# One 512-wide product for the tokens' hi and lo parts in the first layers of an MLP and two FFNs

## The chip, the cores and the metric

The kernel runs on one core of a Trainium2 chip. The metric is the device time of one execution in microseconds. TensorE multiplies (PE in the profile; its weight loads are PEld), VectorE is DVE, ScalarE is ACT, GpSimd is POOL, and SP issues the weights' transfers.

## What is computed

Two transformer blocks on 256 tokens of 1024 features, in float32. The parts of the reference that the change touches are an MLP at the end of the first block and two gated layers (FFNs) at the start and the end of the second:

```python
ff = jnp.square(jax.nn.relu(u2 @ mlp_w1[layer])) @ mlp_w2[layer]      # 1024 -> 4096 -> 1024
h = h + gate2 * ff

def swiglu(x, w_gu, w_down):                                         # 1024 -> 2 x 2816 -> 1024
    g, u = jnp.split(x @ w_gu, 2, axis=-1)
    return (jax.nn.silu(g) * u) @ w_down
x = x + 0.5 * swiglu(rmsnorm(x, ffn1_norm[l]), ffn1_w_gu[l], ffn1_w_down[l])
```

## The kernel before

**Arithmetic.** Each float32 operand of a large product is split into a hi part (rounded to TensorE's fp32r type) and a lo part (the rest). A product of two operands is the sum of three: hi by hi, hi by lo, lo by hi.

**The weight stream.** Class `Stream` brings all weights in order of use, in transfers of at most 2048 columns, into a ring of three raw tiles, and cuts them into pieces of 128 x 1024. A piece's hi part is an ACT copy (L342), its lo part a DVE subtraction (L330). There is room for six split pieces. After each piece of products `done` gives its room back and `fill` splits pieces up to four ahead.

**Order of the work.** Every engine works through its instructions in the order in which the program writes them. TensorE's order is written out by hand. An instruction that needs a tile's buffer waits until the last user of the tile that had it before is done.

**PSUM.** There are eight banks of 512 columns: a0 to a3, w0, w1, t0 and t1. `wbank()` deals out w0 and w1 in turn, `tbank()` t0 and t1 in turn, over the whole program. Five `wbank` calls and an even number of `tbank` calls stand ahead of the MLP.

**The three stages.** In the MLP and in each FFN the first layer gives the hidden features, 128 at a time (one piece of weights), for all 256 tokens; `lin_A` makes a piece from eight blocks of 128 features, three 256-wide products each. Two pieces share a bank: features 2p and 2p + 1 in the MLP, gate and up of one j in an FFN. The pair is then emptied (`relu2`, `hidden`), split into hi and lo, and three pairs (MLP) or four (FFN) later its second-layer products, 512 wide, go into a0 to a3 (`down_tile`, and at the end `down_tail`). The first four pieces (MLP) or two pairs (FFN) of a stage are made the other way round, by `lin_B`, token tile 0 first, into two banks from `wbank()`; their result lies token by token and is transposed behind the stage's first pair, L1369 to L1375 and L1447 to L1454. The head's results in the MLP lie in tiles with the tag `r`, which has two buffers; so does the `r` of `relu2`.

**Work between.** Class `Background` puts small steps of other chains between the products, by a planned clock in microseconds of TensorE that counts 5.2 for a pair and 2.6 for a second-layer piece. In the MLP these are the norm of the memory with four groups of transpositions (`mem_norm`, L1273), in the first FFN the memory's keys (`mem_keys`, two groups, L1324). They take banks from `tbank()`.

**The tokens' parts.** `new_xT` gives two tiles of 128 x 8 x 256, one for the hi parts and one for the lo parts.

Of the kernel before, what the change touches and what calls it, by code (L numbers as in the profile page):

```python
# [16 lines left out]
P = 128  # L17
T = 256
# [7 lines left out]
# the first norm's features come in parts: its shift and scale, then the rows of w_in that take them  # L26
# [3 lines left out]
# ---------------------------------------------------------------- layouts  # L30
# The weights travel as one stream of contiguous pieces, in the order in which
# they are used.  A piece ("sub") is a list of blocks W[128 k : 128 k + 128, c0:c1].
# [4 lines left out]
def _downs(p):  # L37
    """the pairs of hidden pieces whose second product follows the first product of pair p"""
    return [p - 3] * (p >= 3) + [p - 2] * (p == NHID1 // 2 - 1)
# [5 lines left out]
def _plan():  # L45
# [21 lines left out]
    # first block  # L67
# [48 lines left out]
    # second block  # L116
# [31 lines left out]
    # pieces to transfers of at most 2048 columns  # L148
# [22 lines left out]
def _constants():  # L171
# [31 lines left out]
    # ident and ones come first  # L203
# [74 lines left out]
# ---------------------------------------------------------------- the weight stream  # L278
class Stream:
# [46 lines left out]
    def _flush(self):  # L326
        """the lo part of the last piece"""
        if self.pend:
            _, lo, raw, hi = self.pend
            self.nc.vector.tensor_tensor(lo, raw, hi.bitcast(F32), op=OP.subtract)  # L330
            self.pend = None
# [24 lines left out]
    def put(self, t):  # L356
        """the parts of a tile of 1024 columns that is no weight; `drop` gives their room back"""
        assert self.seq - self.released < self.HB
        hi = self.hi_pool.tile([P, 1024], F32R, tag="whi", name=f"ph{self.seq}")
        lo = self.lo_pool.tile([P, 1024], F32R, tag="wlo", name=f"pl{self.seq}")  # L360
        self.nc.scalar.activation(hi, t, AF.Copy)
        self.nc.gpsimd.tensor_tensor(lo, t, hi.bitcast(F32), op=OP.subtract)
        self.seq += 1
        return hi, lo, self.seq - 1
# [15 lines left out]
    def fill(self, la=4, most=3):  # L380
        """splits ahead of the products: at most `la` pieces"""
# [28 lines left out]
def _model(es, tc, nc, x_in, mem_in, wst, sm_in, rows_in, w1_in, cw2_in, sgw_in, posi_in, cst_in, cst1_in, oh_in, out, dbg):  # L410
# [51 lines left out]
    # ------------------------------------------------------------ loads of the start  # L462
# [16 lines left out]
    # ------------------------------------------------------------ ada: acc += W_k c_k  # L479
# [10 lines left out]
    def ada(label, raw):  # L490
        nm, sec, k = label
        c = sc_c[:, k:k + 1]
        if nm == "ada1":
            # a part of the later sums is made on the pool engine
# [30 lines left out]
    # some of the first pieces wait in room of their own  # L525
# [25 lines left out]
    # ------------------------------------------------------------ norms  # L551
    def rstd_of(ssq, n, name, pool=None, scale=None):
        """1/sqrt(ssq*scale + eps) for a small tile."""
# [9 lines left out]
    def split_bank(bank, hi, lo, view=None):  # L563
        """hi and lo of a PSUM bank (ACT and DVE)."""
        src = bank if view is None else view(bank)
        ACT.activation(hi, src, AF.Copy)
        DVE.tensor_tensor(lo, src, hi.bitcast(F32), op=OP.subtract)

    class Norm:
        """the residual's row tile t, normed, as feature-major halves"""  # L570
# [23 lines left out]
        def post(self, h):  # L594
            """out[feature, token] = xn[token, feature] * rstd[token] (+ shift[feature]); returns what makes the lo part"""
# [18 lines left out]

    def new_xT(name, n=8):
        return (xp.tile([P, n, T], F32R, tag="xh", name=f"{name}_h"), xp.tile([P, n, T], F32R, tag="xl", name=f"{name}_l"))

    # ------------------------------------------------------------ linear layers
    def lin_B(labels, ks_of, width, XH, XL, tick=None, mid=None, banks=None, evac=None):
        """out[tok, width] for both token tiles, tile 0 first; labels: subs in order, ks_of[s]: its k tiles"""  # L620
# [32 lines left out]

    def lin_A_pair(la, lb, XH, XL):
# [8 lines left out]
    class Background:  # L663
        """chains of small steps between the linear layers' products.  A chain yields (time of its products,
        time until its next step's operands are there), in us of the tensor engine."""
# [44 lines left out]
    # ============================================================ start  # L710
    ACT.activation(sc_c, S_("c"), AF.Silu)
    # the table of the relative bias, negated
# [3 lines left out]
    # relative bias: its rows over the distance; token p needs them from 1 + p on, key 255 first  # L716
# [5 lines left out]
    # x, normed without its gain, and its transposes  # L722
# [23 lines left out]
    # shift and scale of the first norm as columns, and the products that take them, part by part  # L746
# [3 lines left out]
    def column_sum(parts, h):  # L750
        """the sum over the partitions of half h, on each partition"""
# [76 lines left out]
    # ============================================================ first block: attention  # L828
# [53 lines left out]
    def prep_c():  # L882
        # compressed keys and values
# [11 lines left out]
        for src in range(2):  # L895
            full = b[:, src * 256:src * 256 + 256].rearrange("p (h m) -> p h m", h=2)
            for h in range(2):
                # columns m = 8 c + jp
# [45 lines left out]
    def cmp_attn():  # L944
        # two heads of a group in one product: their keys stand on the diagonal
# [6 lines left out]
        # block c's last key is 16 c + 31  # L952
# [30 lines left out]
    def nsa(lane, tag, units):  # L983
        """units (head, branch) of the selected and the window attention"""
# [85 lines left out]
    # ZT: kc vc ksl kwn g_a q_a; VS: vsl vwn  # L1070
# [60 lines left out]
    debug("ot", OTH.bitcast(F32).rearrange("p a b -> p (a b)"))  # L1131
# [25 lines left out]
    debug("mg", XH.bitcast(F32).rearrange("p a b -> p (a b)"))  # L1157

    def out_proj(nm, XH, XL, resid, gB, shC, name, room):
        """x += (merged @ w), then the normed transposes; token tile 0 first"""  # L1160
# [50 lines left out]
    # ============================================================ two-layer products with the hidden on chip  # L1211
# [12 lines left out]
    def down_tail(labs, Hs, banks, n, resid, gB, name, room):  # L1224
        """the last pieces of the second product, token tile 0 first, and the next norm"""
# [32 lines left out]
    # keys and values of the memory: their products stand between the layers  # L1258
# [47 lines left out]
    def mem_kv(half, between, then):  # L1306
        """one half of mem @ w_kv, and the last norm's rest around it"""
# [21 lines left out]
    # MLP of the first block  # L1329
# [7 lines left out]
    def relu2(p, b):  # L1337
        r = hid.tile([P, 512], F32, tag="r", name=f"r{p}", bufs=2)
        ACT.activation(r, b, AF.Relu)
        DVE.scalar_tensor_tensor(r, b, 0.0, r, op0=OP.max, op1=OP.mult)  # L1340
# [19 lines left out]
    for p in range(2, NHID1 // 2):  # L1360
        b = wbank()
        for i in range(2):
            hi, lo = S.use(("m1", 2 * p + i))
            lin_A(b[:, i * 256:i * 256 + 256], hi, lo, X[0], X[1])
# [11 lines left out]
        relu2(p, b)  # L1376
# [38 lines left out]
    def swiglu(pre, X, mid, gB, name, side=None):  # L1415
# [3 lines left out]
        def hidden(j, b):  # L1419
            r = hid.tile([P, T], F32, tag="r", name=f"{pre}r{j}", bufs=2)  # L1420
            ACT.activation(r, b[:, :256], AF.Silu)  # L1421
            DVE.tensor_tensor(r, r, b[:, 256:512], op=OP.mult)  # L1422
# [17 lines left out]
        for j in range(2, FFT):  # L1440
            b = wbank()
            for i, p in enumerate("gu"):
                hi, lo = S.use((pre, p, j))
                lin_A(b[:, i * 256:i * 256 + 256], hi, lo, X[0], X[1])
# [10 lines left out]
            hidden(j, b)  # L1455
# [9 lines left out]
    # ============================================================ second block  # L1465
# [75 lines left out]
    def spatial():  # L1541
        # layernorm of v
# [105 lines left out]
    def prep2():  # L1648
        # scale columns: the rope part has its gain already
# [5 lines left out]
        # sums of squares; the gates of the last columns come later than this  # L1655
# [50 lines left out]
    def heads():  # L1706
        """keys and queries, transposed, four heads at a time"""
# [104 lines left out]
    debug("ot3", OT3H.bitcast(F32).rearrange("p a b -> p (a b)"))  # L1812
# [60 lines left out]
```

## Time and profile before

| | |
|---|---|
| three runs | 1087.88, 1088.21, 1088.45 us (median 1088.21) |
| span of the profiled execution | 1087.1 us |
| MLP's first pair starts | 284.15 us |
| first FFN's first pair starts | 483.17 us |
| second FFN's first pair starts | 907.11 us |
| busy time of DVE and ACT | 686.3 and 574.0 us |

The profile is that of one execution; its own device time is not listed apart from its span, and the three runs are what it is held against: the median is 1.1 us over the span. In the rows below, times are microseconds from the start of the span. A timeline row has start, duration, engine, line and operation, output <- inputs, the shape, and in brackets the idle time before it and what ended it; equal instructions in a row are merged (x3). In the names ps_w, ps_t and ps_a are the banks w0 and w1, t0 and t1, a0 to a3.

### The profile page before, as it was taken

The page shows a single profiled execution, that of the slowest core. Times are in us where ns is not written, and L with a number is a line of the kernel's source. Part 1 is how long each engine was busy: PE and PEld are TensorE (multiplying, and loading weights), DVE is VectorE, ACT ScalarE, POOL GpSimd, SP SyncE. Part 2 cuts the span into 40 slices and gives each one's busy share as a digit, 9 for nine tenths or more (in the row PEclk, how much of TensorE's full clock was granted, in tenths as well). Part 3 has the DMA queues.
Part 4 walks back from the last instruction along what each step waited for, and adds up shares of the span by engine and source line. Part 5 has one row for each costly group of instructions (what it writes and reads, how often), then busy time and mean ns, then how long its engine had stood idle before and what let it go on. Part 6 is the DMA issues. An engine that isn't in the chain of part 4 may idle for free.

```text
span 1087.1 us, 17034 instructions
## 1 busy us (share of the span) xinstructions
PE 1052.2 (97%) x6973; PEld 953.2 (88%) x6973; DVE 686.3 (63%) x1050; ACT 574.0 (53%) x938; POOL 77.0 (7%) x85
## 2 busy tenths in 40 slices
PE   4899999999999999999999999999999999999998
PEld 2788678898899998889999998889999989999997
DVE  5976767767677664756545556578654876455543
ACT  5257565464664544555444445667566655444441
POOL 4400011120100010000000000000000500000000
PEclk8989999999999999999999999999999999999999
DMA  8685425755566645455555454744333565554551
GB/s 336 255 288 178 175 84 194 266 194 169 222 230 240 260 162 207 168 191 187 188 201 193 156 194 160 236 172 155 117 108 117 204 213 194 194 193 156 194 181 51
DMA packets 31962, 206.09 MB, mean 190 GB/s; under 512 B 3811, under 2 KB 5132, under 8 KB 9996
## 3 DMA queue, kind: packets, MB, share of 16 engines
q1 hardware_dynamic: 30028, 198.74, 50.5%
q0 software_dynamic: 1856, 6.26, 1.8%
q8 instruction: 55, 0.90, 0.3%
q14 instruction: 23, 0.19, 0.0%
HBM read 203.93 MB, written 1.06 MB: 189 GB/s over the span
## 4 chain that ended last, share of the span: by engine, by line
PE 79%; DVE 1%; ACT 1%; issue 0%; ACTq 0%
PE ps_a L455 40%; PE ps_w L455 36%; PE ps_t L455 2%; PE ps_t L561 0%; PE ps_t L1719 0%; DVE wl L330 0%; PE ps_w L1752 0%; PE ps_t L1791 0%; DVE u_l L612 0%; PE ps_t L1575 0%; ACT u_h L608 0%; PE ps_t L1536 0%; ACT wh L342 0%; PE ps_t L1451 0%; ACT GT L1809 0%
## 5 line engine op out<-in xcount | busy, mean ns | idle before, releaser
L330 DVE TENSOR_TENSOR wl<-raw,wh 128x1024 fp32r<-128x1024 f32 (+2 forms) x331 | 393.5, 1226 | 78.8 <-ACT wh L342 78.2
L342 ACT ACTIVATE wh<-raw 128x1024 fp32r<-128x1024 f32 (+2 forms) x331 | 325.6, 1029 | 16.9 <-DMA raw<-in_wst_dram 6.5
L455 PE MATMUL ps_w<-x_h,wh 128*128 128x256 f32 x640 | 181.2, 283 | 0.0
L455 PE MATMUL ps_w<-x_h,wl 128*128 128x256 f32 x640 | 181.1, 283 | 0.0
L455 PE MATMUL ps_w<-x_l,wh 128*128 128x256 f32 x640 | 181.1, 283 | 0.0
L455 PEld LDWEIGHTS ps_w<-x_h,wh 128*128 128x128 f32 x640 | 122.7, 192 | 1.4
L455 PEld LDWEIGHTS ps_w<-x_l,wh 128*128 128x128 f32 x640 | 122.7, 192 | 1.3
L455 PEld LDWEIGHTS ps_w<-x_h,wl 128*128 128x128 f32 x640 | 122.7, 192 | 0.0
L455 PE MATMUL ps_w<-u_h,wh 128*128 128x256 f32 x224 | 63.4, 283 | 0.0
L455 PE MATMUL ps_w<-u_l,wh 128*128 128x256 f32 x224 | 63.4, 283 | 0.0
L455 PE MATMUL ps_w<-u_h,wl 128*128 128x256 f32 x224 | 63.4, 283 | 0.0
L455 PE MATMUL ps_a<-hmix_h,wh 128*128 128x256 f32 x192 | 57.1, 297 | 0.0
L455 PE MATMUL ps_a<-u_h,wh 128*128 128x256 f32 x192 | 56.5, 294 | 0.0
L455 PE MATMUL ps_a<-hmix_l,wh 128*128 128x256 f32 x192 | 54.3, 283 | 0.0
L455 PE MATMUL ps_a<-hmix_h,wl 128*128 128x256 f32 x192 | 54.2, 282 | 0.0
L455 PE MATMUL ps_a<-u_l,wh 128*128 128x256 f32 x192 | 54.2, 282 | 0.0
L455 PE MATMUL ps_a<-u_h,wl 128*128 128x256 f32 x192 | 54.2, 282 | 0.0
L455 PE MATMUL ps_a<-wh,hh 128*128 128x512 f32 x128 | 50.3, 393 | 0.0
L455 PE MATMUL ps_a<-wl,hh 128*128 128x512 f32 x128 | 50.1, 391 | 0.1
L455 PE MATMUL ps_a<-wh,hl 128*128 128x512 f32 x128 | 49.9, 390 | 0.0
L1421 ACT ACTIVATE f2r<-ps_w 128x256 f32<-128x256 f32 x20 | 7.7, 385 | 78.1 <-PE ps_w L455 78.1
L1422 DVE TENSOR_TENSOR f2r<-f2r,ps_w 128x256 f32<-128x256 f32 x20 | 8.4, 422 | 62.1 <-ACT f2r L1421 62.1
(494 smaller groups left out, 2408.1 us busy)
## 6 DMA issues: line engine op xcount, KB each, us to landing
raw<-in_wst_dram SPq DMA_DIRECT2D x170, 1024.0 KB, 4.9
raw<-in_wst_dram SPq DMA_DIRECT2D x9, 768.0 KB, 4.3
raw<-in_wst_dram SPq DMA_DIRECT2D x4, 792.0 KB, 8.3
raw<-in_wst_dram SPq DMA_DIRECT2D x3, 512.0 KB, 10.8
xr<-in_x_dram SPq DMA_DIRECT2D x2, 512.0 KB, 4.8
cw<-in_w_dram POOLq DMA_DIRECT2D x1, 1024.0 KB, 5.2
NB<-Dr SPq DMA_DIRECT2D x1, 1024.0 KB, 10.2
f<-in_rows_dram POOLq DMA_DIRECT2D x2, 512.0 KB, 4.4
```

What stands on the lines that cost most here:

```text
L330: self.nc.vector.tensor_tensor(lo, raw, hi.bitcast(F32), op=OP.subtract)
L342: self.nc.scalar.activation(hi[:, :w], raw, AF.Copy)
L455: PE.matmul(o, l, r, start=start, stop=stop, skip_group_check=True)
L1421: ACT.activation(r, b[:, :256], AF.Silu)
L1422: DVE.tensor_tensor(r, r, b[:, 256:512], op=OP.mult)
```

## The change

`new_xT` makes one tile in which each feature block's hi and lo parts lie side by side. In the first layers of the three stages each block's hi weights multiply both parts in one 512-wide product, and the lo weights multiply the hi part into the bank's first half. A piece now fills a bank of its own. `fold` empties it: ACT copies the second half into an SBUF tile, DVE adds the first half. The banks are dealt out by `fbank()`: w0, w1, t0, t1 in turn. The rest of the diff takes out comments and four debug lines.

```diff
+    class Halves(tuple):
+        def __new__(cls, tile):
+            self = tuple.__new__(cls, (tile[:, :, 0], tile[:, :, 1]))
+            self.both = tile
+            return self
+
     def new_xT(name, n=8):
-        return (xp.tile([P, n, T], F32R, tag="xh", name=f"{name}_h"), xp.tile([P, n, T], F32R, tag="xl", name=f"{name}_l"))
+        return Halves(xp.tile([P, n, 2, T], F32R, tag="x", name=name))
...
+    def lin_wide(b, hi, lo, X):
+        for k in range(KD):
+            sl = slice(k * P, (k + 1) * P)
+            mm(b, hi[:, sl], X.both[:, k].rearrange("p a q -> p (a q)"), k == 0, False)
+            mm(b[:, 0:T], lo[:, sl], X[0][:, k], False, k == KD - 1)
+
+    def fbank():
+        return rot("w0", "w1", "t0", "t1")
+
+    def fold(dst, b):
+        ACT.activation(dst, b[:, T:2 * T], AF.Copy)
+        DVE.tensor_tensor(dst, b[:, 0:T], dst, op=OP.add)
...
-    def relu2(p, b):
-        r = hid.tile([P, 512], F32, tag="r", name=f"r{p}", bufs=2)
-        ACT.activation(r, b, AF.Relu)
-        DVE.scalar_tensor_tensor(r, b, 0.0, r, op0=OP.max, op1=OP.mult)
+    def relu2(p, r):
+        DVE.scalar_tensor_tensor(r, r, 0.0, r, op0=OP.max, op1=OP.mult)
...
     for p in range(2, NHID1 // 2):
-        b = wbank()
+        r = hid.tile([P, 512], F32, tag="r", name=f"r{p}", bufs=2)
         for i in range(2):
             hi, lo = S.use(("m1", 2 * p + i))
-            lin_A(b[:, i * 256:i * 256 + 256], hi, lo, X[0], X[1])
+            b = fbank()
+            lin_wide(b, hi, lo, X)
+            fold(r[:, i * T:i * T + T], b)
             S.done(("m1", 2 * p + i))
             S.fill()
...
-        relu2(p, b)
+        relu2(p, r)
...
-        def hidden(j, b):
-            r = hid.tile([P, T], F32, tag="r", name=f"{pre}r{j}", bufs=2)
-            ACT.activation(r, b[:, :256], AF.Silu)
-            DVE.tensor_tensor(r, r, b[:, 256:512], op=OP.mult)
+        def hidden(j, g, u):
+            ACT.activation(g, g, AF.Silu)
+            DVE.tensor_tensor(u, g, u, op=OP.mult)
+            r = u
...
         for j in range(2, FFT):
-            b = wbank()
-            for i, p in enumerate("gu"):
+            gu = []
+            for p in "gu":
                 hi, lo = S.use((pre, p, j))
-                lin_A(b[:, i * 256:i * 256 + 256], hi, lo, X[0], X[1])
+                b = fbank()
+                lin_wide(b, hi, lo, X)
+                gu.append(hid.tile([P, T], F32, tag=p, name=f"{pre}{p}{j}", bufs=2))
+                fold(gu[-1], b)
                 S.done((pre, p, j))
                 S.fill()
...
-            hidden(j, b)
+            hidden(j, *gu)
```

## Rows read from the trace of the kernel before

**Rows 1.** The page's first part: busy time, share of the span and instructions.
```profile
PE 1052.2 (97%) x6973; PEld 953.2 (88%) x6973; DVE 686.3 (63%) x1050; ACT 574.0 (53%) x938; POOL 77.0 (7%) x85
```

**Rows 2.** Busy time by stretches: stretch, length, PE, PEld, DVE, ACT, POOL, clock, DMA.
```profile
580.00:600.00 20.00, 20.00 (x143) 18.83 (x142) 11.07 (x13) 9.96 (x13) 0.00 (x0) 1.00 0.47 171
```

**Rows 3.** The page's costliest groups: busy us, mean ns of one, idle before.
```profile
L455 PE MATMUL ps_w<-x_h,wh 128*128 128x256 f32 x640 | 181.2, 283 | 0.0
...
L1421 ACT ACTIVATE f2r<-ps_w 128x256 f32<-128x256 f32 x20 | 7.7, 385 | 78.1 <-PE ps_w L455 78.1
L1422 DVE TENSOR_TENSOR f2r<-f2r,ps_w 128x256 f32<-128x256 f32 x20 | 8.4, 422 | 62.1 <-ACT f2r L1421 62.1
```

**Rows 4.** Timeline of PE: 512-wide products from the first, 256-wide from the second.
```profile
500.87 0.40 PE L455 MATMUL ps_a<-wh,f1hh 128*128 128x512 f32 x1
...
503.61 0.28 PE L455 MATMUL ps_w<-x_h,wh 128*128 128x256 f32 x1
...
509.37 0.40 PE L455 MATMUL ps_a<-wh,f1hh 128*128 128x512 f32 x1
```

**Rows 5.** Timeline at the gate's column sum behind the MLP's pair 14.
```profile
422.71 0.69 DVE L1340 SCALAR_TENSOR_TENSOR r<-ps_w,r 128x512 f32<-128x512 f32 x1 [6.57 <-ACT r L1339]
...
423.46 0.50 PE L455 MATMUL ps_w<-ph,onesr 128*128 128x512 f32 x1 [1.01 <-DVE r L1340]
```

**Rows 6.** Timeline at the start of the MLP: PE, DVE and ACT.
```profile
284.15 0.28 PE L455 MATMUL ps_w<-u_h,wh 128*128 128x256 f32 x1
...
289.90 1.04 PE L561 MATMUL ps_t<-cst,rh 128*128 128x128 f32 x8
...
284.98 0.69 DVE L1356 SCALAR_TENSOR_TENSOR rh<-ps_w,rh 128x512 f32<-128x512 f32 x1 [2.41 <-ACT rh L1355]
...
291.83 0.76 DVE L567 TENSOR_TENSOR hl<-ps_t,hh 128x256 fp32r<-128x256 f32 x2 [0.45 <-ACT hh L566]
...
284.84 2.94 ACT L342 ACTIVATE wh<-raw 128x1024 fp32r<-128x1024 f32 x3
290.54 0.38 ACT L566 ACTIVATE hh<-ps_t 128x256 fp32r<-128x256 f32 x1 [2.75 <-PE ps_t L561]
```

**Rows 7.** Timeline at the start of the first FFN: PE, DVE and ACT.
```profile
483.17 0.28 PE L455 MATMUL ps_w<-x_h,wh 128*128 128x256 f32 x1
...
488.92 0.60 PE L1451 MATMUL ps_t<-cst,f1rh 128*128 128x128 f32 x4
489.27 0.37 PE L455 MATMUL ps_w<-x_h,wh 128*128 128x256 f32 x1
...
483.78 0.42 DVE L1436 TENSOR_TENSOR f1rh<-f1rh,ps_w 128x256 f32<-128x256 f32 x1 [2.18 <-ACT f1rh L1435]
...
490.85 0.42 DVE L567 TENSOR_TENSOR f1hl<-ps_t,f1hh 128x256 fp32r<-128x256 f32 x1 [0.45 <-ACT f1hh L566]
...
489.56 0.38 ACT L566 ACTIVATE f1hh<-ps_t 128x256 fp32r<-128x256 f32 x1 [2.96 <-PE ps_t L1451]
```

**Rows 8.** Timeline at the memory's second group of transpositions: PE and ACT.
```profile
341.89 0.60 PE L561 MATMUL ps_t<-cst,memt 128*128 128x128 f32 x4
...
342.09 0.60 ACT L1339 ACTIVATE r<-ps_w 128x512 f32<-128x512 f32 x1 [3.37 <-PE ps_w L455]
```

**Rows 9.** Idle stretches of PE in the timeline, then stretches with their granted clock.
```profile
42.55 0.35 PE L455 MATMUL ps_t<-cst,first 128*128 128x1 f32 x2 [1.78 <-DVE first L509]
55.89 0.35 PE L455 MATMUL ps_t<-cst,first 128*128 128x1 f32 x2 [3.87 <-DVE first L509]
109.49 0.76 PE L1007 MATMUL ps_w<-cst,ns 128*128 128x128 f32 x3 [2.10 <-DVE ns L1003]
...
43.00:46.00 3.00, 3.00 (x21) 2.73 (x21) 1.96 (x5) 0.64 (x2) 1.36 (x2) 1.00 0.98 409
56.00:63.00 7.00, 7.00 (x25) 6.21 (x26) 4.14 (x10) 3.27 (x5) 0.28 (x1) 0.51 0.58 243
110.00:115.00 5.00, 4.78 (x18) 3.52 (x18) 4.89 (x10) 2.85 (x5) 0.00 (x0) 0.66 0.54 206
```

More of the change, by code (lines that the diff above doesn't have):

```diff
@@ L1130, in _model @@
     bg.drain()
-    debug("ot", OTH.bitcast(F32).rearrange("p a b -> p (a b)"))
     XH, XL = new_xT("mg")
@@ L1156, in _model @@
     split_to(XH, XL, 7, SG[:, 7, 0])
-    debug("mg", XH.bitcast(F32).rearrange("p a b -> p (a b)"))
     def out_proj(nm, XH, XL, resid, gB, shC, name, room):
@@ L1811, in _model @@
     bg.drain()
-    debug("ot3", OT3H.bitcast(F32).rearrange("p a b -> p (a b)"))
     XH, XL = new_xT("mg2")
```

## The prediction, made before the change was run

> **What bounds the kernel now.** I read the page's busy times first, then the busy time by stretches, then the stretches of the MLP and the two FFNs in order of time on TensorE, and last what ScalarE (ACT) and VectorE (DVE) do where such a stage begins. TensorE is busy 97% of the span [rows 1]; in a stretch inside an FFN it is busy 20.00 of 20.00 us at granted clock 1.00, while DVE has 11.07 and ACT 9.96 us [rows 2]. So there the end is set by how fast products start one behind the other. The "283 ns" of a product [rows 3] is its latency in the pipeline; the pace is the distance of two starts. Forty-eight 256-wide products start between 503.61 and 509.37: 0.1200 us each. Twelve 512-wide ones start between 500.87 and 503.61: 0.2283 us each [rows 4]. No gap stands between them, so whatever TensorE saves here the kernel saves, and whatever TensorE is made to wait here it loses.
>
> **What the change removes.** Per block of 128 features the first layer has three 256-wide products, 3 x 0.1200 = 0.3600 us. After the change it has one 512-wide and one 256-wide, 0.2283 + 0.1200 = 0.3483 us: as many columns, one product and one weight load fewer, 0.0117 us less. It applies to 28 pieces of the MLP and 2 x 20 pieces of each FFN, 108 pieces of 8 blocks, 864 blocks: 864 x 0.0117 = 10.1 us. The two widths leave a surcharge per product: (0.2283 - 0.1200)/256 = 0.42 ns per column, so a product costs some 12 ns beside its columns. What the rows don't show is a 512-wide and a 256-wide product in turn; from the two rates the saving is bounded by 0 (the wide one pays the surcharge twice) and 2 x 12 ns x 864 = 20 us (the product behind a wide one pays none). I take 10.1, since each row's own rate holds whatever stands next to it.
> A rule speaks against even this. The Trainium skill, "TensorE: Matmul & The Clock Gate", section "Wait — 56ns, not 53.3ns?", says that back-to-back products start N / 2.4 GHz plus about 2.5 ns apart; by it the change would save 2.5 ns x 864 = 2.2 us. The rows of this kernel differ from it, 120 and 228 ns where it gives 109 and 216, so the sum goes by the rows.
>
> **What it adds beside TensorE.** Each piece gets a fold, an ACT copy of half a bank (like L1421, 385 ns) and a DVE sum (like L1422, 422 ns) [rows 3]. Per pair of an FFN, some 8.5 us, that is 0.77 us of ACT and 0.84 us of DVE, about 9 and 10% of their time, over the 50 and 55% of [rows 2]. They are hidden while the pieces that TensorE multiplies next are split early enough. The fold stands ahead of the piece's fill on ACT's queue, so the split of the weights four pieces on now waits for the end of this piece and the fold, where before it ran as soon as ACT was free. It is still done about 0.2 + 0.4 + 1.0 + 1.2 = 2.8 us behind the piece's end, and it is needed three pieces later, at least 8.2 us. So I cost it at nothing; its transfers on SP's queue move by the same distance and keep their distance to the splits. If that cover is gone, TensorE waits at a piece's start. X's hi and lo parts lie in one tile now; if a product that reads hi must wait for the DVE step that writes lo beside it, that is one step of at most 0.69 us (as L1356, 512 columns [rows 6]) at the starts of the three stages. The parts are read one at a time, as before, so I take 0.
>
> **Where TensorE waits for a bank.** This is the step that decides. The pieces no longer alternate between w0 and w1, they go w0, w1, t0, t1; the count is 28, then 68, so each of the three stages begins at w0 and its second pair lies in t0 and t1. But t0 and t1 also serve the transpositions, and w0 and w1 the stage's first product (its token tile 0 in w1, tile 1 in w0: five such banks were taken before the MLP, and an even number in between). A bank is given to its next user when its last reader is done. That this wait is real stands in the trace: the column sum at 423.46 waited 1.01 us for L1340's reading of its bank, and the product started 0.06 us behind the reader's end at 422.71 + 0.69 = 423.40 [rows 5]. So, with E for the time at which TensorE could go on:
> (a) First piece of each stage in w0, just left by tile 1. Before it went to w1, empty for long. MLP: E = 284.15, DVE reads until 284.98 + 0.69 = 285.67, start 285.73: 1.6 us [rows 6]. First FFN: E = 483.17, DVE until 483.78 + 0.42 = 484.20: 1.1 us [rows 7]; the second FFN is the same, 1.1 us. Sum 3.8.
> (b) Third piece (second pair) of each FFN in t0, where the transposed first hidden tiles lie. E is behind the four transpositions, 489.27. Their evacuation takes two ACT and two DVE steps in turn, since they wait for one another, from 489.56 to 490.85 + 0.42 = 491.27: 1.71 us [rows 7]. In the changed order ACT has the fold and one split ahead of it. The fold starts 0.20 us behind the last product (as ACT does at 342.09 after 341.89, [rows 8]); 0.28 us later the split, 0.95 us later the evacuation (three splits take 2.94 us [rows 6]); so it ends 0.20 + 0.28 + 0.95 + 1.71 = 3.14 us behind the piece, the product starts at 3.2, and TensorE, which has 0.35 us of transpositions, waits 2.9 us. Twice: 5.7.
> (c) The same in the MLP, where it is longer. The tile r of pair 2 is now taken before its pieces, and the two buffers of that tag still hold the head's results until they are transposed behind piece 5. So both folds, with the split between and the one behind them, start only when the first transpositions are done, 290.54 - 289.90 = 0.64 us behind the last piece [rows 6]. Then 2 x (0.28 + 0.95) = 2.5 us, and the evacuation of t0, from 290.54 to 291.83 + 0.42 = 1.71 us: 4.9 with the start. TensorE has eight transpositions, 0.8 us, and waits 4.1 us. If the tiles did not hold it up it would be 2.4.
> (d) Transpositions of the memory into t1 right behind a pair that has just used t1: at 341.89 [rows 8] and 365.27 in the MLP, and at 526.36 in the first FFN. Each waits for the fold of the piece that has just ended: ACT 0.20 us behind it, DVE 0.41 later for 0.42, start 0.06 later: 1.1 us. Sum 3.3. Those that follow a pair in w0 and w1 wait for nothing.
> Together 3.8 + 5.7 + 4.1 + 3.3 = 16.9 us. The gate's column sum behind pair 14 waits for a fold instead of L1340: about the same 1.0 us as before.
>
> **The clock.** TensorE idled 1.78 us before 42.55 and the granted clock stayed 1.00; it idled 2.10 us before 109.49 and 3.87 before 55.89, and fell: the mean clock was 0.66 over 110 to 115 and 0.51 over 56 to 63 [rows 9], which is 1.2 instead of 2.4 GHz for a while and costs (1 - 0.66) x 5 = 1.7 and 3.4 us. The new idle stretches of 4.1, 2.9 and 2.9 us are of that size. Dense products stand on both sides of them, where those at 109.49 were thin, so I take two falls of three, 1.7 us each: 3.4. Bounds: 0, and 3.4 + 2 x 1.7 = 6.8.
>
> **Sum.** The profiled span is 1087.1, the runs' median 1088.21, 1.1 us more, which lies around the span and stays. 1088.2 - 10.1 + 16.9 + 3.4 = 1098.4 us, 0.9% slower.
>
> **Rivals.**
> A. The waits are there but short: ACT's order leaves (c) at 2.4, the clock doesn't fall. 1088.2 - 10.1 + 15.2 = 1093.3.
> B. The banks are empty when they are met, because my count of their turns is wrong at the stages' starts: then only (d) is left and the saving shows, 1088.2 - 10.1 + 3.3 = 1081.4. For it: the trace doesn't name bank numbers. Against it: the wait at 423.46.
> C. On the other side too, by one mechanism: the weight load is the limit, at each of the 864 blocks. For it: PEld is busy 18.83 of 20 us [rows 2]. A block would then cost its columns, 768 x 0.42 = 0.325 us, and save 0.035 x 864 = 30 us: 1088.2 - 30 + 20.3 = 1078.5. It decides from 20.3/864 = 24 ns saved per block on. Against it: 512-wide products, each with twice the time for its load, pay the same surcharge as narrow ones. The Trainium skill, "Perfetto Trace Analysis", section "Identifying the Most-Contended Engine", would point here, since it judges TensorE by the busy share of the weight loads.
> D. The surcharge goes with the columns, nothing is saved: 1088.2 + 20.3 = 1108.5. The skill's 2.5 ns would give 1106.3. Against both: [rows 4].
> E. The folds hold the splits up so long that TensorE waits at pieces' starts all along: 0.2 us at each of 108 pieces is 22 us more, 1120. Against it: DVE and ACT are little over half busy.
>
> **How the numbers follow.** Forecast 0.66, A 0.14, B 0.07, C 0.03, D 0.03, E 0.04, a balance near zero 0.03. A measurement of this kernel can tell about 0.2% from no change, 2.2 us. Faster: B and C, 0.10. Within: 0.04. Slower: 0.86. The range takes in the forecast with its clock bounds (1095.0 to 1101.8), A, and the merged tile's 3 x 0.7 us: 1091 to 1104.
>
> **What would show it.** Right: 512- and 256-wide starts 0.348 us apart per block; TensorE idle before the third piece of each stage (about 4, 3, 3 us, released by DVE's reading of a transposed bank), before the first (1.1 to 1.6 us), and 1.1 us at three transpositions; half clock behind some. Wrong: no idle of over 0.5 us there, or a block at 0.325 or 0.36 us, or waits of pieces on the splits of their weights.

## The result, and the profile after

The changed kernel takes 1112.41 us (median of four runs, 1110.23 to 1114.52), the kernel before 1088.16 beside it: a ratio of 1.0225, 95% interval [1.0208, 1.0243]. The change makes it 24 us slower, where 10 us slower was forecast and 1104 was the range's end. The profiled execution took 1114.52 us around a span of 1112.8.

First the page of the changed kernel, beside [rows 1] and [rows 3]: busy times, and its costliest groups in the first layers (busy us, mean ns of one, idle before).

```profile
PE 1059.6 (95%) x6109; PEld 913.9 (82%) x6109; DVE 734.9 (66%) x1158; ACT 602.6 (54%) x1032; POOL 77.0 (7%) x85
...
L455 PE MATMUL ps_t<-x,wh 128*128 128x512 f32 x320 | 116.7, 406 | 6.2 <-DVE f2hl L567 3.5
L455 PE MATMUL ps_w<-x,wh 128*128 128x512 f32 x320 | 113.8, 398 | 1.9 <-DVE f2rh L1457 0.9
```

864 products are gone (6973 to 6109), and TensorE is busy 7.4 us longer. New is the last column: the wide products wait, behind the transposed hidden tiles (f2hl) above all.

The timeline of TensorE shows every stop, that is, every stretch in which it idles ahead of a product; these are all of at least 0.4 us from the MLP to the end of the second FFN's first layer, but one that both kernels have in the attention (0.43 us). In brackets stands the idle time ahead of the product, and what released it. Before, there was one of 1.01 us [rows 5].

```profile
287.27 0.50 PE L455 MATMUL ps_w<-u,wh 128*128 128x512 f32 x1 [1.41 <-DVE rh L1375]
297.97 0.77 PE L455 MATMUL ps_t<-u,wh 128*128 128x512 f32 x1 [3.90 <-DVE hl L567]
347.82 0.50 PE L455 MATMUL ps_t<-u,wh 128*128 128x512 f32 x1 [1.91 <-DVE memT_l L567]
356.15 0.66 PE L561 MATMUL ps_t<-cst,memt 128*128 128x128 f32 x4 [0.94 <-DVE r L675]
380.79 0.66 PE L561 MATMUL ps_t<-cst,memt 128*128 128x128 f32 x4 [0.93 <-DVE r L675]
437.92 0.50 PE L455 MATMUL ps_w<-ph,onesr 128*128 128x512 f32 x1 [0.93 <-DVE r L675]
442.49 0.50 PE L455 MATMUL ps_a<-wl,hh 128*128 128x512 f32 x1 [0.40 <-DVE wl L330]
499.38 0.50 PE L455 MATMUL ps_w<-x,wh 128*128 128x512 f32 x1 [0.93 <-DVE f1rh L1457]
508.41 0.47 PE L455 MATMUL ps_t<-x,wh 128*128 128x512 f32 x1 [2.68 <-DVE f1hl L567]
547.91 0.66 PE L561 MATMUL ps_t<-cst,km 128*128 128x128 f32 x4 [1.41 <-DVE f1u L675]
672.09 0.50 PE L455 MATMUL ps_a<-wl,f1hh 128*128 128x512 f32 x1 [0.73 <-DVE wl L330]
929.16 0.50 PE L455 MATMUL ps_w<-x,wh 128*128 128x512 f32 x1 [0.93 <-DVE f2rh L1457]
939.07 0.77 PE L455 MATMUL ps_t<-x,wh 128*128 128x512 f32 x1 [3.54 <-DVE f2hl L567]
```

Together they are 20.6 us against 1.0. Each stop costs somewhat more than its idle time, because a product's busy time reaches past the moment at which the next could have started: 0.28 us busy at a pace of 0.12 [rows 3, 4], so 0.16 us per stop behind a 256-wide product.

Next the clock: four stretches of the changed kernel, each behind one of the four longest stops (stretch, length, PE, PEld, DVE, ACT, POOL, granted clock, DMA share, GB/s).

```profile
297.00:304.00 7.00, 6.03 (x19) 5.19 (x20) 3.72 (x7) 2.19 (x6) 0.00 (x0) 0.52 0.47 152
348.00:352.00 4.00, 4.00 (x15) 3.43 (x16) 2.03 (x2) 0.00 (x0) 0.00 (x0) 0.57 0.26 45
508.00:513.00 5.00, 4.59 (x17) 3.97 (x18) 2.16 (x4) 0.53 (x2) 0.00 (x0) 0.66 0.25 103
939.00:943.00 4.00, 3.93 (x14) 3.39 (x15) 0.68 (x2) 0.42 (x1) 0.00 (x0) 0.57 0.61 244
```

Here 1.2 instead of 2.4 GHz was granted for part of the time: 0.48 x 7 + 0.43 x 4 + 0.34 x 5 + 0.43 x 4 = 8.5 us of clock withheld. In the first stretch the fall begins inside the 3.90 us stop, which is counted already; from the product at 297.97 to 304.12 the clock is 0.50, 3.1 us lost instead of 3.4. So the clock costs 8.2 us beside the idle time. Elsewhere between the MLP and the end of that list it is 1.00, or within a slice at the edges of these stretches.

Last the pace, in the timeline inside the first FFN: a wide and a narrow product in turn.

```profile
579.72 0.28 PE L455 MATMUL ps_t<-x,wl 128*128 128x256 f32 x1
579.84 0.40 PE L455 MATMUL ps_t<-x,wh 128*128 128x512 f32 x1
...
582.20 0.28 PE L455 MATMUL ps_t<-x,wl 128*128 128x256 f32 x1
```

Seven blocks from 579.72 to 582.20: 0.354 us each; over 560 to 640 us the means are 0.236 from a wide start to a narrow one and 0.117 back, 0.353 in all. That is 0.007 less than the 0.3600 of before, 6.0 us in 864 blocks.

So of the span's growth of 25.7 us: -6.0 of pace, +19.6 idle, +8.2 clock, about +1.9 for twelve more stops of 0.16, and 1.1 that was there before the changed code is reached (the product ps_w<-cst,ns of [rows 9], "the ns product" from here on, stands at 110.61 us, before at 109.49). That makes 24.8; stops shorter than 0.4 us are not in it.

### The profile page after: what moved, and what is told of

Read it like the earlier page. It is cut to its first block, busy times and chain, and to the rows that moved or that the text cites. A ratio compares the mean times of both kernels' runs of the same rounds, so it can differ in the third digit from the quotient of the medians.

```text
span 1112.8 us, 15586 instructions
## 1 busy us (share of the span) xinstructions
PE 1059.6 (95%) x6109; PEld 913.9 (82%) x6109; DVE 734.9 (66%) x1158; ACT 602.6 (54%) x1032; POOL 77.0 (7%) x85
## 4 chain that ended last, share of the span: by engine, by line
PE 74%; DVE 3%; ACT 3%; issue 1%; ACTq 0%
PE ps_a L455 37%; PE ps_w L455 21%; PE ps_t L455 15%; DVE wl L330 1%; ACT wh L342 1%; PE ps_t L561 0%; PE ps_t L1743 0%; DVE r L675 0%; DVE acc L513 0%; PE ps_w L1776 0%; PE ps_t L1815 0%; DVE u L612 0%; ACT r L674 0%; DVE r L1359 0%; DVE memT_l L567 0%
## 5 line engine op out<-in xcount | busy, mean ns | idle before, releaser
L455 PE MATMUL ps_t<-x,wh 128*128 128x512 f32 x320 | 116.7, 406 | 6.2 <-DVE f2hl L567 3.5
L455 PE MATMUL ps_w<-x,wh 128*128 128x512 f32 x320 | 113.8, 398 | 1.9 <-DVE f2rh L1457 0.9
L455 PE MATMUL ps_t<-x,wl 128*128 128x256 f32 x320 | 91.1, 285 | 0.0
L455 PE MATMUL ps_w<-x,wl 128*128 128x256 f32 x320 | 89.7, 280 | 0.0
L455 PEld LDWEIGHTS ps_t<-x,wh 128*128 128x128 f32 x320 | 61.6, 193 | 21.7 <-issue 6.6
L455 PEld LDWEIGHTS ps_w<-x,wh 128*128 128x128 f32 x320 | 60.1, 188 | 17.1 <-DVE f2rh L1457 1.4
L455 PE MATMUL ps_a<-hmix,wh 128*128 128x256 f32 x384 | 72.8, 290 | 0.0
L455 PE MATMUL ps_a<-u,wh 128*128 128x256 f32 x384 | 72.2, 288 | 0.0
L455 PEld LDWEIGHTS ps_t<-x,wl 128*128 128x128 f32 x320 | 61.9, 193 | 0.7
L455 PEld LDWEIGHTS ps_w<-x,wl 128*128 128x128 f32 x320 | 60.4, 189 | 0.6
```

The costliest lines, as they stand in the source:

```text
L455: PE.matmul(o, l, r, start=start, stop=stop, skip_group_check=True)
```

## Experiments

Theory: the loss is TensorE waiting for t0, t1 and w0, which others have not emptied, and half clock behind these waits; the wide product itself is a gain. Rivals: the wide product or the fold is at fault; the splits are held up; the waits would move rather than go. All diffs are against the changed kernel. The time up to the ns product, where no kernel differs in what it computes, was between 104.9 and 111.1 us in the profiles, so differences below some 4 us are read from the traces behind that point: "the rest" below is the distance from that product's start to the start of the last product (973.2 us in the kernel before, 997.8 in the changed one).

### Two banks, heads in a room of their own

```
 def fbank():
-    return rot("w0", "w1", "t0", "t1")
+    return rot("w0", "w1")
...
 def head(t, b):
-    r = hid.tile([P, 512], F32, tag="r", name=f"rh{t}", bufs=2)
+    r = room[:, t * 512:(t + 1) * 512]
```

> The wide product is kept; the pieces rotate over w0 and w1 alone (t0 and t1 are left to the transposes), and the MLP's two head results stand in room1 instead of the two r tiles, so that the folds of the first pieces need not wait for the transposes of the heads. My theory (the loss is idle time behind banks that another step has not emptied, 18 to 19 us by the trace of the changed kernel, and 8 to 9 us of half clock behind it; the wide product itself saves 0.0065 us per block, 5.6 us in 864): no idle interval of TensorE above 0.5 us is left in the MLP and the FFNs but the memory's column sum, granted clock 1.00 in every 20 us window of them, 1082.6 us (1081 to 1085), faster than the kernel before. Rival (the half clock comes from the wide products or from the folds' own lateness, not from the banks): a clock near 0.9 stays behind the heads, or waits of about 1 us appear between the pieces, 1090 us or more.

1082.57 us, ratio 0.9941 [0.9924, 0.9958]; the rest 969.0. The timeline of TensorE has three stops of over 0.45 us left in these stages:

```profile
421.09 0.49 PE L455 MATMUL ps_w<-ph,onesr 128*128 128x512 f32 x1 [0.47 <-DVE r L675]
425.66 0.50 PE L455 MATMUL ps_a<-wl,hh 128*128 128x512 f32 x1 [0.77 <-DVE wl L330]
647.99 0.50 PE L455 MATMUL ps_a<-wl,f1hh 128*128 128x512 f32 x1 [0.72 <-DVE wl L330]
```

The clock behind the heads, where the changed kernel had half of it, in stretches of this kernel:

```profile
300.00:320.00 20.00, 20.00 (x104) 16.94 (x104) 16.85 (x24) 12.05 (x19) 0.00 (x0) 1.00 0.75 261
500.00:520.00 20.00, 20.00 (x107) 17.03 (x106) 12.22 (x18) 13.81 (x22) 0.00 (x0) 1.00 0.59 205
940.00:960.00 20.00, 20.00 (x107) 17.09 (x106) 12.70 (x18) 10.04 (x16) 0.00 (x0) 1.00 0.53 175
```

With the same wide products and folds, the idle time, the half clock and 30 us of time are gone, and the kernel is 0.6% faster than the one before. The banks (with the r tiles) are the cause; the product and the fold are not. The stops that wait for a split were expected to be absent and are there, 0.77 and 0.72 us.

### The heads' room alone, with four banks

```
-    r = hid.tile([P, 512], F32, tag="r", name=f"rh{t}", bufs=2)
+    r = room[:, t * 512:(t + 1) * 512]
```

> The changed kernel, with one edit: the MLP's two head results stand in room1 instead of the two r tiles. My theory: the wait for the MLP's transposed heads falls from 3.90 to 2.4 to 2.7 us, as in the FFNs (2.68 and 3.54), all other idles stay; 1109 to 1111 us (1112.4 - 1.3, and up to 1.7 less where the clock no longer falls). Rival (the r tiles don't matter, the bank t0 alone does): 3.9 us stay, 1112.4.

1108.84 us, ratio 1.0183 [1.0165, 1.0201]; the rest 994.8, 3.1 below the changed kernel. The timeline of TensorE at the three places:

```profile
285.33 0.50 PE L455 MATMUL ps_w<-u,wh 128*128 128x512 f32 x1 [1.41 <-DVE room L1375]
294.37 0.47 PE L455 MATMUL ps_t<-u,wh 128*128 128x512 f32 x1 [2.24 <-DVE hl L567]
343.00 0.63 PE L455 MATMUL ps_t<-u,wh 128*128 128x512 f32 x1 [1.90 <-DVE memT_l L567]
```

3.90 fell to 2.24, a little under the 2.4 to 2.7 that I expected, and the others stayed. Of the 3.1 us, 1.7 are this idle time and 1.4 the clock, whose fall behind the heads costs 1.7 us here instead of 3.1. The r tiles' 1.66 us are seen in the changed kernel's own timeline of ACT, where the first fold waits for the transposition of the heads (released by ps_t L561), and the evacuation hh (ACT's copy of a transposed bank, which empties it together with DVE's subtraction hl) stands behind two folds and two splits:

```profile
293.67 0.38 ACT L674 ACTIVATE r<-ps_w 128x256 f32<-128x256 f32 x1 [6.23 <-PE ps_t L561]
293.95 1.05 ACT L342 ACTIVATE wh<-raw 128x1024 fp32r<-128x1024 f32 x1
294.89 0.38 ACT L674 ACTIVATE r<-ps_w 128x256 f32<-128x256 f32 x1
295.16 1.05 ACT L342 ACTIVATE wh<-raw 128x1024 fp32r<-128x1024 f32 x1
296.11 0.38 ACT L566 ACTIVATE hh<-ps_t 128x256 fp32r<-128x256 f32 x1
```

### Grouped: eight wide products, then eight narrow ones

Two banks and the room as above, and:

```
         for k in range(KD):
-            sl = slice(k * P, (k + 1) * P)
-            mm(b, hi[:, sl], X.both[:, k].rearrange("p a q -> p (a q)"), k == 0, False)
-            mm(b[:, 0:T], lo[:, sl], X[0][:, k], False, k == KD - 1)
+            mm(b, hi[:, k * P:(k + 1) * P], X.both[:, k].rearrange("p a q -> p (a q)"), k == 0, False)
+        for k in range(KD):
+            mm(b[:, 0:T], lo[:, k * P:(k + 1) * P], X[0][:, k], False, k == KD - 1)
```

> As the run with two banks and the heads in room1, but each piece does its eight 512-wide products first and its eight 256-wide ones behind them, where the changed kernel alternates them. The changed kernel's block takes 0.353 us where 0.2283 + 0.1200 = 0.3483 was summed from rows of before. Theory of the alternation (a product of one width behind one of the other pays more): block 0.348, 1088.2 - 10.1 = 1078 us, 4 to 5 below the two-bank run. Rival (the price stands on the wide product with this tile or on the columns): block 0.353 again, the same time as the two-bank run within 1 us.

1077.95 us, ratio 0.9908 [0.9891, 0.9924]; the rest 964.9, 4.1 below the two-bank kernel that alternates. The timeline of TensorE inside the first FFN, where eight equal products stand in one line:

```profile
560.10 2.00 PE L455 MATMUL ps_w<-x,wh 128*128 128x512 f32 x8
561.94 1.11 PE L455 MATMUL ps_w<-x,wl 128*128 128x256 f32 x8
562.89 0.40 PE L455 MATMUL ps_a<-wh,f1hh 128*128 128x512 f32 x1
```

Eight wide ones take 1.84 us and eight narrow ones 0.95: 0.2300 + 0.1188 = 0.349 per block. The sum of the rates of [rows 4], 0.3483, holds if products of one width follow each other; taken in turn they cost 0.004 to 0.005 us more per block.

### By twos

As the last, with two wide and two narrow products in turn.

> As the run with two banks, but two 512-wide products, then two 256-wide ones, four times per piece. Alternated, a block takes 0.3530 us (0.2357 from a wide product's start to a narrow one's, 0.1170 back), grouped by eights 0.3488 (1.84 us for eight wide, 0.95 for eight narrow). Theory (the price stands on each change of width): by twos half of it is paid, 0.351 per block, 1080.5 us, between the two-bank run (1082.6) and the grouped one (1078.0). Rival (any run of two or more products of one width is enough): 0.3488, 1078.

1075.99 us, ratio 0.9889 [0.9863, 0.9914]; the rest 964.2. The timeline of TensorE:

```profile
580.26 0.63 PE L455 MATMUL ps_w<-x,wh 128*128 128x512 f32 x2
580.73 0.39 PE L455 MATMUL ps_w<-x,wl 128*128 128x256 f32 x2
...
583.04 0.63 PE L455 MATMUL ps_w<-x,wh 128*128 128x512 f32 x2
```

Eight blocks from 580.26 to 583.04, 0.348 each. The theory of a price on each change of width fell (it asked for 0.351); two products of one width in a row are enough to be rid of it, in the sum of a block. By twos and by eights can't be told apart: their rests differ by 0.7 us. These two are the fastest versions measured, about 1% below the kernel before.

### The narrow product into the bank's right half

Two banks and the room, alternating, and:

```
-    mm(b[:, 0:T], lo[:, sl], X[0][:, k], False, k == KD - 1)
+    mm(b[:, T:2 * T], lo[:, sl], X[0][:, k], False, k == KD - 1)
```

> As the run with two banks, alternating, but the lo weights' 256-wide products are added into the right half of the bank instead of the left (the fold adds the halves, so the sum is the same). The narrow product then writes columns that the wide one before it wrote last, and the next wide one starts on columns that the narrow one did not touch. Theory (the price of 0.0045 us per block is one of the change of width itself): block 0.353 and 1082.6 us again, within 1. Rival (it is one of the columns that are written again soon after): the block moves by 0.002 us or more, in either direction, 2 us or more of time.

1084.17 us, ratio 0.9953 [0.9935, 0.9971]; the rest 969.1 against 969.0 with the left half. Means over 560 to 640 us are 0.2355 from a wide start to a narrow one and 0.1172 back: 0.353 again. The median lies 1.6 us above the two-bank kernel's, more than the 1 us expected, but the pace and the rest are the same. So the price of alternating doesn't depend on which half of the bank the narrow product writes. What it is remains open.

### The banks without the wide product

```
-    mm(b, hi[:, sl], X.both[:, k].rearrange("p a q -> p (a q)"), k == 0, False)
+    mm(b[:, 0:T], hi[:, sl], X[0][:, k], k == 0, False)
+    mm(b[:, 0:T], hi[:, sl], X[1][:, k], False, False)
...
-    ACT.activation(dst, b[:, T:2 * T], AF.Copy)
-    DVE.tensor_tensor(dst, b[:, 0:T], dst, op=OP.add)
+    ACT.activation(dst, b[:, 0:T], AF.Copy)
+    DVE.tensor_tensor(dst, b[:, 0:T], dst, op=OP.max)
```

> The changed kernel's banks and evacuations without its wide product: each piece makes the 24 256-wide products of the kernel before in one half of a bank, in the rotation over w0, w1, t0 and t1, and is emptied by a copy on ScalarE and an operation on VectorE of the fold's size (a maximum, so that the sum is not doubled). My theory: the same idles at the same places as in the changed kernel (1.4, 3.9, 1.9, 0.9, 0.9; 0.9, 2.7, 1.4; 0.9, 3.5; each within 0.4), the same falls of the clock, and no saving: 1112.4 + 5.6 = 1118 us (1114 to 1120). Rival (the waits need the wide product's shorter pieces or its fold over both halves): idles under 0.5 us, 1088 to 1093 us.

1117.2 us, ratio 1.0266 [1.0247, 1.0285]. The stops stand where the changed kernel has them; three of its timeline of TensorE:

```profile
298.51 0.77 PE L455 MATMUL ps_t<-u,wh 128*128 128x256 f32 x2 [3.90 <-DVE hl L567]
510.40 0.47 PE L455 MATMUL ps_t<-x,wh 128*128 128x256 f32 x2 [2.68 <-DVE f1hl L567]
941.86 0.47 PE L455 MATMUL ps_t<-x,wh 128*128 128x256 f32 x2 [3.54 <-DVE f2hl L567]
```

All are within 0.2 us of those above. So the change is two changes of opposite sign: the banks cost 29 us with 24 narrow products per piece (1117.2 against 1088.6 of the kernel before beside it), and the wide product then saves 5. The clock did not fall as expected in all places: none follows the 2.68 us stop here. The rests differ by 4.6 us (1002.4 against 997.8); with the 1.7 of that fall it is 6.3, the pace's saving.

### Narrow products, two banks

The last kernel's products and folds with the two banks and the room.

> The kernel with 24 256-wide products per piece and the fold's two operations (a copy and a maximum), with two banks and the heads in room1: the pieces and folds of the change without its wide product and without its t0 and t1. My theory: a piece per bank and the two operations that empty it cost TensorE nothing, so the two runs with four banks and the two with two banks differ by the same: 1082.6 + 6 = 1088.2 us (1087 to 1090), the time of the kernel before, with no idle above 0.8 us in the MLP and the FFNs. Rival (the folds fill ScalarE and VectorE and delay the splits): 1091 or more, with idles at products that wait for a split.

1089.07 us, ratio 1.0002 [0.9989, 1.0016]; the rest 975.1, 6.1 above the two-bank kernel with the wide product: the saving of 864 x 0.007 by itself. Its stops are 0.47, 0.76 (wl) and 0.72 (wl), as with the wide product. Against the kernel before, whose rest is 973.2, a piece per bank and the fold cost about 1.5 us at the two places where the next splits then come late, and little else.

### t1 ahead of t0

```
-    return rot("w0", "w1", "t0", "t1")
+    return rot("w0", "w1", "t1", "t0")
```

> The changed kernel with its rotation turned in one place: w0, w1, t1, t0 in place of w0, w1, t0, t1. The order in which the kernel takes its banks is plain from its code: the FFNs' transposed heads stand in t0, the MLP's in t0 and then t1, the memory's first transposes in t0, the next three steps' in t1, t0, t1, those of the keys in f1 in t1 and t0. My theory (each idle belongs to one bank and to what was put into it last): a piece now meets t0 one piece, 2.8 us, later, so in f1 2.68 goes to 0 and in f2 3.54 to about 0.7; the memory's 1.91 and both 0.94 in the MLP go to 0; the MLP's 3.90 grows to about 5.2, because t1 is emptied behind t0; the 1.41, 0.93 and 0.93 at the first pieces and 0.93 at the column sum stay. Idle 21 us to about 12, and three falls of the clock of 1.8 us each less: 1112.4 - 9 - 5 = 1098 us (1095 to 1102). Rival (whatever comes first behind the heads waits, for the folds or the splits are late, not for a bank): the idles stay as they were, 1112 us.

1093.97 us, ratio 1.0042 [1.0025, 1.0059]; the rest 981.5, 16.3 below the changed kernel. Of its timeline of TensorE:

```profile
297.65 0.77 PE L455 MATMUL ps_t<-u,wh 128*128 128x512 f32 x1 [5.11 <-DVE hl L567]
...
925.88 0.47 PE L455 MATMUL ps_t<-x,wh 128*128 128x512 f32 x1 [0.77 <-DVE f2hl L567]
```

Between the two stand only 0.93, 0.40, 0.93, 0.73 and 0.93, at the places that should keep them, and the 0.43 of the attention. 3.90 grew to 5.11, 3.54 fell to 0.77, and 1.91, 0.94, 0.93, 2.68 and 1.41 are gone. Each wait follows the bank, not the place in the program, and a piece that meets the bank 2.8 us later finds it empty or nearly so. The time came out 1 us below the low end of what I expected, with one fall of the clock left, in the MLP, of which 2.2 us lie behind the stop.

### w1 ahead of w0

```
-    return rot("w0", "w1", "t0", "t1")
+    return rot("w1", "w0", "t0", "t1")
```

> The changed kernel with the rotation w1, w0, t0, t1: each stage's first piece goes into the bank of the heads' first token tile instead of the second's. My theory: the 1.41, 0.93 and 0.93 at the first pieces vanish, and the 0.93 at the column sum (its first bank is now one piece older) falls to 0.5 or less; the waits in t0 and t1 stay as they are. Idle 21 to about 17.4, 1112.4 - 3.7 = 1108.7 us (1106 to 1111). Rival (a wait removed ahead of the third piece only makes the third piece wait longer): 3.90, 2.68 and 3.54 each grow by the 0.9 to 1.4 won, 1112 us.

1102.8 us, ratio 1.0133 [1.0115, 1.0151]; the rest 989.1, 8.7 below the changed kernel, where 3.7 was expected. The idle times did as said: none at the three first pieces, 0.47 at the column sum, and 3.90, 2.68 and 3.54 unchanged, so nothing moved on to the third pieces; only the wait for wl behind the column sum grew, from 0.40 to 0.75. The other 5 us are the clock's. Two stops in the timeline of TensorE, then the stretches behind them:

```profile
341.19 0.50 PE L455 MATMUL ps_t<-u,wh 128*128 128x512 f32 x1 [1.91 <-DVE memT_l L567]
...
499.05 0.47 PE L455 MATMUL ps_t<-x,wh 128*128 128x512 f32 x1 [2.68 <-DVE f1hl L567]
```
```profile
341.00:345.00 4.00, 3.81 (x21) 3.35 (x22) 2.61 (x4) 0.98 (x3) 0.00 (x0) 1.00 0.20 31
499.00:503.00 4.00, 3.95 (x23) 3.50 (x24) 2.22 (x4) 1.31 (x3) 0.00 (x0) 1.00 0.19 78
```

Behind the same 1.91 and 2.68 us the clock stayed at 1.00 here, and behind 3.90 it cost 1.7 us instead of 3.1. With 1.7 each for the two falls that are absent that is 4.8 us. Why the clock did not fall was not tested.

### The r tiles, with two banks

By twos, with two banks, and the heads back in the r tiles.

> The by-twos kernel with two banks, and the MLP's head results back in the two r tiles, as in the changed kernel. With four banks that edit alone moved the wait behind the MLP's transposed heads from 2.24 to 3.90 us. My theory: with two banks the third piece goes into w1, whose fold must wait until the transposes of the first head tile (0.77 us) have read the r tile; the fold then takes about 0.9 us, the transposes of the second tile 0.77: 0.3 to 1.2 us of idle time at the third piece, no fall of the clock, 1076.0 + 0.8 = 1076.8 us (1075 to 1079). Rival (the r tiles cost 1.7 us wherever the banks are, and the clock falls behind that): an idle of 1.7 us and 1.7 us of half clock, 1079.4 us.

1079.94 us, ratio 0.9920 [0.9899, 0.9941]; the rest 965.6, 1.4 above the kernel by twos with the room. One stop is new in the timeline of TensorE, and the clock stays at 1.00 around it:

```profile
290.60 0.74 PE L455 MATMUL ps_w<-u,wh 128*128 128x512 f32 x2 [0.49 <-DVE r L676]
```

The shared tile costs 0.49 us of idle time with two banks, 1.66 with four. The time lies 0.9 us above the range expected, near the rival's 1079.4, but its 1.7 us of idle time and its fall of the clock are absent. The medians' difference of 4 us is not the tile's price: in the profiles 3.6 us lie ahead of the ns product, and of the 1.4 behind it 0.6 lie ahead of the heads' transpositions, which the edit doesn't reach.

## Why the prediction was wrong in size

**The mechanism and the sign were right.** The waits were forecast at E, when TensorE could go on, so they compare with the idle time plus what is left of the last product or transposition (0.16 us behind a 256-wide product, about 0.25 behind transpositions). First pieces (a): 1.57, 1.09 and 1.09 against 1.6, 1.1 and 1.1. The first FFN's third piece (b): 2.93 against 2.9. The MLP's (c): 4.1 against 4.1, and without the r tiles 2.5 against 2.4. The memory's two transpositions (d): 1.1 against 1.1. Costing a wait as the end of the bank's last reader plus 0.06 us [rows 5], with the reader's queue written out step by step, held within 0.1 us for these eight, and the rotation of the banks was counted rightly. Rivals B and A fell with that.

**The saving was mis-sized: 6.0 us, not 10.1.** The step said that each row's own rate holds whatever stands next to it. The run by eights and the run by twos show that the sum holds where neighbours of the same width stand together (0.349 and 0.348 per block against 0.3483); in turn the block is 0.353. The bounds that were kept, 0 and 20, held it. Rivals C (0.325 per block) and D (0.360) fell by the same rows.
The 2.5 ns per product of the Trainium skill, "TensorE: Matmul & The Clock Gate", section "Wait — 56ns, not 53.3ns?", would have given an estimate of 2.2 us. No order of the products here agrees with it: by eights, 230 and 119 ns from start to start were measured for 512 and 256 columns.

**The waits' sum was 5.0 us short.** 21.9 us by the rows above, counted at E, against 16.9.
- The sum had the transpositions that wait for a piece in t1, and the heads' bank, but of the memory's first transpositions it only said that those which follow a pair in w0 and w1 wait for nothing. That is so; but the piece behind them waits, in the t0 that they have just filled: 1.91 us idle at 347.82, 2.2 us. A shared bank has two directions of waiting, and I went through one. How long such a wait is depends on the reader's queue: ACT had a table load of 1.28 us ahead of this evacuation, which started 3.9 us behind the transpositions (342.55). The third group of transpositions fills t0 in the same way at 370.52, its evacuation starts 2.2 us later with no table load ahead, and the piece behind it waited 0.16 us. That the table load makes the difference is read from these rows of ACT and TensorE, not tested:

```profile
343.88 1.28 ACT L1323 ACT_TABLE_LOAD   x1
346.47 0.58 ACT L566 ACTIVATE memT_h<-ps_t 128x512 fp32r<-128x512 f32 x1
...
374.04 0.50 PE L455 MATMUL ps_t<-u,wh 128*128 128x512 f32 x1 [0.16 <-DVE memT_l L567]
```

- The second FFN was taken as the first. There DVE has a split of 1.23 us between ACT's first copy of the evacuation and its own subtraction: 3.54 idle, 3.8 instead of 2.9. The rows are of the changed kernel's timeline of ACT and DVE:

```profile
936.35 0.38 ACT L566 ACTIVATE f2hh<-ps_t 128x256 fp32r<-128x256 f32 x1
936.49 1.23 DVE L330 TENSOR_TENSOR wl<-raw,wh 128x1024 fp32r<-128x1024 f32 x1 [0.52 <-ACT wh L342]
937.63 0.42 DVE L567 TENSOR_TENSOR f2hl<-ps_t,f2hh 128x256 fp32r<-128x256 f32 x1
```

- The transposition in the first FFN (d) waited 1.41 us, 1.6 at E, not 1.1: DVE had started a split of 1.22 us at 546.30, so the fold's sum began at 547.44, where ACT's copy, started at 546.59, takes about 0.4.
- The splits were costed at nothing. At two places, behind the column sum late in the MLP and behind the last pair of the first FFN, TensorE waits 0.40 and 0.73 us for wl, 1.4 at E. Rival E named this mechanism, but for all 108 pieces; it is at two, and the run with narrow products and two banks shows that it comes with the pieces and folds and needs neither the wide product nor t0 and t1 (0.76 and 0.72 there).

**The clock was mis-sized: 8.2 us, not 3.4.** The price per fall was right for three of the four, 1.7 us (0.43 x 4, 0.34 x 5). The number was wrong: I took two falls of three. In this profile all the long stops had one, the one at 347.82 too that I had not listed, and behind the MLP's the clock stayed low longer, 3.1 us. The bound of 6.8 did not hold it, since it counted falls for three stops only.

In sum 1098.4 + 4.1 + 5.0 + 4.8 = 1112.3, against 1112.41 measured. That it comes so close is in part luck: the terms are read from the profiled execution, which took 1114.52, and of those 2.2 us more only 1.1 are found, ahead of the changed code. The range failed because its upper end added bounds to the terms that were listed and nothing for a wait that was not, while one such wait costs 2.2 us and its fall of the clock 1.7 more.

## What to carry to other kernels

A change that makes products cheaper and puts them into banks that other steps use is two changes: price them apart, and leave the banks out if the old ones do (here a loss of 24 us then becomes a gain of 6, and of 11 to 14 with products of one width next to each other; behind the ns product, where the change acts, the gains are 4 and 8 to 9). For each shared bank go through its uses in order and cost every pair of neighbours, whichever of the two comes first, with what stands ahead in the reader's queue. And give each new stop like those here, of 1.9 us and more amid dense products, its own fall of the clock in the range's upper end.

## What the runs showed of the hardware

- Products of two widths in strict turn (512, 256, 512, ...) cost 0.353 us per pair, in runs of two or eight of a width 0.348: about 5 ns per pair, at the step from the wide to the narrow (0.236 against 0.230), with part of it given back at the next (0.117 against 0.119). Which half of the bank the narrow one writes makes no difference (0.353 either way). The cause is open.
- Stops of the same length are not always followed by half clock. Behind 3.5 us and more it fell in each profile that has such a stop; behind 2.68 in two of four, behind 2.24 in the one that has it, behind 1.9 in three of four; behind 1.41 and less never in these stages. Behind 3.90 and 5.11 it cost 2.2 to 3.1 us in the three profiles with a stop of 1.41 us ahead, where it fell before the stop was over, and 1.7 us in the one without. When it falls is not settled by these runs. Two falls more or less, 3.4 us, would be most of the spread of the changed kernel's times (1110.2 to 1114.5); that they are the reason was not tried.
- The stretch ahead of the changed code took between 104.9 and 111.1 us in twelve profiles of the same work, with granted clocks between 0.69 and 1.00 in its 20 us stretches. A few us between two medians need the trace behind that stretch before they are read as an edit's effect.
